# RG-LRU heads in pairs with 64x64 gate products, and mLSTM chunks with grouped products, in a two-layer mixer trunk

## The chip, the cores and the metric

One NeuronCore of a Trainium2 chip runs the whole program. The metric is the device time of one execution in microseconds (us). PE is the matrix engine (its weight loads are listed as PEld), DVE the vector engine, ACT the scalar engine, POOL and SP issue DMAs. Each engine runs its instructions in the order that the build fixed.

## The reference

A trunk of two layers over 768 tokens (256 of context, 512 latent), width 1024, in float32. In each layer one projection feeds three bidirectional mixers (HGRN2, mLSTM, RG-LRU), whose outputs are gated, merged, projected and followed by a SwiGLU FFN. The change lies in the RG-LRU (8 blocks of 64 features) and in the mLSTM (4 heads), both cut here:

```
def rglru(xc, r_pre, i_pre, lam, h0):
    log_a = -LRU_C * jax.nn.softplus(-lam) * jax.nn.sigmoid(r_pre)
    a = jnp.exp(log_a)
    u = jnp.sqrt(jnp.maximum(-jnp.expm1(2.0 * log_a), 0.0)) * (jax.nn.sigmoid(i_pre) * xc)
    a_cum, h = lax.associative_scan(_linear_combine, (a, u), axis=1)
...
    xc = depthwise_conv(lru_x, conv_w, conv_b).astype(f32)
    gates = jnp.einsum('btnd,zgnde->zgbtne', xc.reshape(bsz, t, LRU_BLOCKS, LRU_BD),
                       lru_gate_w.astype(f32)).reshape(N_DIR, 2, bsz, t, LRU_W)
...
        log_d = jnp.where(mask, b[..., :, None] - b[..., None, :] + ic[..., None, :], NEG_BIG)
...
        s = jnp.einsum('bhtk,bhsk->bhts', qc, kc) * jnp.exp(log_d - m_row[..., None])
        w_inter = jnp.exp(log_inter - m_row)
        num = s @ vc + w_inter[..., None] * (qc @ c_mem)
        den = jnp.sum(s, axis=-1) + w_inter * jnp.einsum('bhtk,bhk->bht', qc, n_mem)
        h = num / jnp.maximum(jnp.abs(den), jnp.exp(-m_row))[..., None]
...
    b_out = head_rms_norm(h_ml, ml_norm_w) * jax.nn.sigmoid(ml_o.astype(f32))
    c_out = h_lru * jax.nn.gelu(lru_y.astype(f32))
```

## The kernel before

Activations are kept feature-major, 128 features by 768 tokens. A dense product takes its weights from DRAM (SP's queue, 512 KB a panel), splits them into a high part on ACT (`split_w`, L210) and a low part on DVE (L212), and runs three PE products per 128 rows (L386 for the mixers' projections, L496 token-major, L1050 in the later stages) in one of four accumulation banks of PSUM (`acc`). Two banks (`mx`) and two more (`pl`) serve the mixers. In a layer the stages follow as: HGRN2 heads, RG-LRU heads (`lru(i)`, four of 128 features), mLSTM gates and log-decays (`mg`), mLSTM head pairs (`mlstm(0)`, `mlstm(1)`), branches, output, FFN. The framework's scheduler fixes the order of each engine at build time by its own estimates, and mixes work of neighbouring stages: projections of the next stage stand on PE between the small products of the one before. Buffers are rings by tag (`BUFS`), and the order of an instruction among others follows from what it reads and from `high_priority`.

`lru(i)` projects x (L788), convolves it on DVE (L791, L795), fills a 128x128 block-diagonal tile with two 64x64 blocks per direction and gate (a memset, two DMAs), and multiplies: per direction and gate one product of 512 and one of 256 columns (L808), each emptied by a sigmoid on ACT (L809). Then Exp (L815), Tanh (L816) and Sqrt (L824) on ACT, each from another function table, multiplications (L817, L819, L820, L825) and the scans (L827, L829, L830) on DVE, and the gelu of y.

`mg` projects values and gates, transposes the gates (L885), scans them over time on DVE (L888 to L892), and transposes three results to columns (L923); the first waits for L900. Log-decays go to DRAM.

`mlstm(p)` treats two heads: keys weighed by column (L954), state products (L973, 64 columns each) and the states (L980). Then for each 128-token chunk: log-decays are loaded (`ub`), shifted and masked (L992) and exponentiated (L994); scores (L998, 64 rows) are weighed with them (L1001); for each head and direction a product of weighed scores and values (L1008, 128 rows) and one with the state (L1010, 64 rows) add up in a bank. ACT takes the absolute denominator (L1013) and scales (L1017), DVE does the rest (L1014, L1015, L1018). `head_norm_out` then normalizes each head over all chunks (L629 to L635), transposes (L640) and gates it.

## Time and profile before

| | |
|---|---|
| median of three runs | 2617.3 us (2615.47 to 2621.12) |
| the profiled execution | 2623.0 us, span 2621.2 us, mean granted clock 0.983 |
| PE busy | 2540.6 us, 97% of the span |
| DVE, ACT, POOL busy | 1573.5, 962.8, 111.1 us |
| chain that ended last | PE 49%, issue 4%, DVE 4%, DMA 1%, ACT 1% |

A line of the profile names an operation by its source line, its engine and the tiles that it writes and reads; L0lru_pl is a `pl` bank in layer 0's RG-LRU. A busy share says how full an engine is; what a change of one stage can move is read from the waits of that stage.

### The profile page before, as it was taken

The numbers are of one execution on the slowest core, as the hardware profiler recorded it, in microseconds if no ns is written. First come the engines' busy times: TensorE is split into PE (matmuls) and PEld (weight loads), VectorE is DVE, ScalarE is ACT, GpSimd is POOL, SyncE is SP. The second block draws the span as 40 slices with busy tenths as digits, with TensorE's granted clock in tenths as the row PEclk, the third lists the DMA queues.
The fourth block names the chain that finished last, engine by engine and source line by source line (L and its number), as shares of the span: only waits on it lengthen the run. The fifth ranks groups of instructions, "written<-read, shape, count | busy, mean of one in ns | idle before, by whom it ended". The sixth has DMA issues, their size and how long they took to land.

```text
span 2621.2 us, 36224 instructions
## 1 busy us (share of the span) xinstructions
PE 2540.6 (97%) x14491; PEld 2195.9 (84%) x14491; DVE 1573.5 (60%) x3007; ACT 962.8 (37%) x1470; POOL 111.1 (4%) x213
## 2 busy tenths in 40 slices
...
GB/s 243 57 48 54 46 69 65 75 77 105 142 128 114 120 121 145 112 99 167 113 103 139 51 139 65 57 55 64 63 80 122 112 105 176 114 97 97 97 91 111
DMA packets 247480, 264.42 MB, mean 101 GB/s; under 512 B 12328, under 2 KB 213360, under 8 KB 247312
## 3 DMA queue, kind: packets, MB, share of 16 engines
...
## 4 chain that ended last, share of the span: by engine, by line
PE 49%; issue 4%; DVE 4%; DMA 1%; ACT 1%; POOL 0%; ACTq 0%; DVEq 0%; POOLq 0%
PE L0ffn_acc L1050 18%; PE L1ffn_acc L1050 14%; PE L1br_acc L1050 5%; PE L1hg_acc L386 4%; PE L1mg_acc L496 1%; PE L1hg_pl L707 1%; PE L1ml_acc L386 1%; PE L1lru_acc L386 1%; PE L1out_acc L1050 1%; PE L1v_acc L496 1%; PE L1lru_pl L808 0%; PE L1ml_mx L1010 0%; DVE L0ffn_h L377 0%; PE L1hg_mx L746 0%; DMA L1hg_w<-in_w_in_dram 0%
## 5 line engine op out<-in xcount | busy, mean ns | idle before, releaser
L1050 PE MATMUL L0ffn_acc<-L0out_h,L0ffn_wh 128*128 128x256 f32 (+1 forms) x1408 | 349.3, 340 | 6.7 <-DVE L0out_h L377 3.0
L1050 PEld LDWEIGHTS L0ffn_acc<-L0out_h,L0ffn_wh 128*128 128x128 f32 x1408 | 242.0, 190 | 39.1 <-DVE L0out_h L377 4.4
L1050 PE MATMUL L0ffn_acc<-L0out_h,L0ffn_wl 128*128 128x256 f32 (+1 forms) x704 | 236.4, 337 | 0.0
L1050 PE MATMUL L1ffn_acc<-L1out_h,L1ffn_wh 128*128 128x512 f32 (+1 forms) x736 | 219.7, 381 | 1.8 <-ACT L1out_h L376 0.9
L258 DVE SCALAR_TENSOR_TENSOR ada_ny<-ada_w,csk,ada_ny 128x512 f32<-128x512 f32 x224 | 157.8, 749 | 74.9 <-DMA ada_w<-in_w_ada_dram 73.9
L1050 PE MATMUL L0br_acc<-h,L0br_wh 128*128 128x512 f32 (+1 forms) x768 | 191.3, 340 | 0.3 <-DVE L0br_gt L1099 0.3
L210 ACT ACTIVATE L0ffn_wh<-L0ffn_w 128x1024 fp32r<-128x1024 f32 (+1 forms) x76 | 77.3, 1017 | 278.4 <-PE L0ffn_acc L1050 250.6
L212 DVE TENSOR_TENSOR L1ffn_wl<-L1ffn_w,L1ffn_wh 128x1024 fp32r<-128x1024 f32 (+1 forms) x76 | 88.8, 1169 | 142.2 <-ACT L1ffn_wh L210 141.3
L1050 PE MATMUL L0ffn_acc<-L0ffn_hid,L0ffn_wh 128*128 128x256 f32 (+1 forms) x704 | 172.5, 337 | 0.0
L1050 PEld LDWEIGHTS L1ffn_acc<-L1out_h,L1ffn_wh 128*128 128x128 f32 x736 | 136.2, 188 | 28.8 <-DVE L1out_h L377 1.5
L210 ACT ACTIVATE L1ffn_wh<-L1ffn_w 128x1024 fp32r<-128x1024 f32 (+1 forms) x76 | 77.4, 1018 | 197.5 <-PE L1ffn_acc L1050 156.8
L212 DVE TENSOR_TENSOR L0ffn_wl<-L0ffn_w,L0ffn_wh 128x1024 fp32r<-128x1024 f32 (+1 forms) x68 | 81.1, 1192 | 111.6 <-ACT L0ffn_wh L210 111.1
L1050 PEld LDWEIGHTS L0br_acc<-h,L0br_wh 128*128 128x128 f32 x768 | 131.9, 190 | 17.3 <-DVE L0br_gt L1099 0.5
L1050 PEld LDWEIGHTS L0ffn_acc<-L0out_h,L0ffn_wl 128*128 128x128 f32 x704 | 133.4, 190 | 14.3
L1050 PE MATMUL L1ffn_acc<-L1out_h,L1ffn_wl 128*128 128x512 f32 (+1 forms) x368 | 139.4, 380 | 0.0
L386 PE MATMUL L0hg_acc<-h,L0hg_wh 128*128 128x384 f32 (+2 forms) x512 | 136.1, 343 | 0.0
L1050 PEld LDWEIGHTS L0ffn_acc<-L0ffn_hid,L0ffn_wh 128*128 128x128 f32 x704 | 121.0, 190 | 14.2
L1050 PE MATMUL L0br_acc<-h,L0br_wl 128*128 128x256 f32 (+1 forms) x384 | 129.5, 337 | 0.0
L1050 PE MATMUL L1br_acc<-L0ffn_h,L1br_wh 128*128 128x512 f32 x384 | 121.0, 393 | 1.5 <-ACT L1br_gt L1069 1.5
L1050 PE MATMUL L1ffn_acc<-L1ffn_hid,L1ffn_wh 128*128 128x512 f32 (+1 forms) x448 | 115.2, 346 | 0.0
L386 PE MATMUL L1hg_acc<-L0ffn_h,L1hg_wh 128*128 128x384 f32 (+1 forms) x384 | 107.8, 359 | 0.0
L1050 PE MATMUL L0ffn_acc<-L0ffn_hid,L0ffn_wl 128*128 128x256 f32 (+1 forms) x304 | 102.2, 336 | 0.0
(707 smaller groups left out, 5932.4 us busy)
## 6 DMA issues: line engine op xcount, KB each, us to landing
...
```

The lines of the kernel that those rows point to most:

```text
L210: ACT.activation(wh[:, :n], w[:, :n], AF.Copy)
L212: V.tensor_tensor(wl[:, :n], w[:, :n], wh[:, :n].bitcast(F32), op=OP.subtract)
L258: V.scalar_tensor_tensor(ac[i], wv, csk[:, kk, i:i + 1], ac[i], op0=OP.mult, op1=OP.add)
L386: PE.matmul(ps[:, :n], A[:, k, :], B[k][:, off - ao:off - ao + n], start=(i == 0), stop=(i == 3 * nk - 1))
L496: PE.matmul(ps[:, :n], A[k][:, c * 128:(c + 1) * 128], W[:, k % 4, :], start=k == 0 and i == 0, stop=k == 7 and i == 3 * (k1 - k0) - 1)
L707: PE.matmul(pv[:, j * 128:(j + 1) * 128], ks[:, j * 128:(j + 1) * 128], comp(Q[g], c, j, j + 1), start=True, stop=True)
L1050: PE.matmul(ps[:, :n], A[:, k, sl], Bm[k0 + k][:, off - ao:off - ao + n], start=cnt[key] == 0, stop=cnt[key] == tot - 1)
```

## The change

`lru` now takes two heads. Pair (0,1) stands where the four heads stood, pair (2,3) behind `mg` and ahead of the mLSTM. The 64x64 gate blocks are multiplied as such: for the first gate two products on the diagonal quadrants of the array, for the second two on the other two, with the conv's output whose halves two DMAs have swapped (`xs`); both gates of a direction and column group have a bank. All sigmoids of a pair come first, then Exp, Tanh and squares, then Sqrt (`behind` fixes the order without a wait). a² and a step of the gelu go from DVE to ACT.

In `mlstm` the weights of three chunks are prepared ahead in tiles of other tags; the 64-row state products of both heads are written ahead of the 128-row products, and the next chunk's scores between them; the absolute value and the scaling go from ACT to DVE; each head is normalized in two halves, the first while later chunks run. The tile P becomes T wide.

```
+    def behind(ins, other):
+        tc.add_manual_dep(ins.ins, other.ins.name, mybir.DependencyInfo(mybir.DependencyClass.NoSync, mybir.DependencyReason.DATA),
+                          reason="issue order")
...
+                xs = S("kt")
+                wg = S("th", 256).rearrange("p (z c) -> p z c", z=4)
+                for b in range(2):
+                    ldg(xs[64 * b:64 * b + 64], xc[64 - 64 * b:128 - 64 * b])
+                    for z in range(2):
+                        ldg(wg[64 * b:64 * b + 64, z::2, :], gw[:, z, 2 * i + (1 - b if z else b)].rearrange("d n e -> n d e"))
+                sg[i] = [[S(t) for t in ts] for ts in ((("K", "K"), ("K", "K")), (("P", "P"), ("z", "Q")))[k]]
+                for d in range(2):
                     for off, n in ALL:
-                        ps = pl()
-                        PE.matmul(ps[:, :n], wg[:, 2 * d + z], xc[:, off:off + n], start=True, stop=True)
-                        ACT.activation(sg[d][z][:, off:off + n], ps[:, :n], AF.Sigmoid, bias=vec[l]["gate_b"][:, bi:bi + 1])
+                        pz = [pl() for z in range(2)]
+                        for b in range(2):
+                            PE.matmul(pz[0][64 * b:64 * b + 64, :n], wg[64 * b:64 * b + 64, 2 * d], xc[64 * b:64 * b + 64, off:off + n],
+                                      start=True, stop=True)
+                        for b in range(2):
+                            PE.matmul(pz[1][64 - 64 * b:128 - 64 * b, :n], wg[64 * b:64 * b + 64, 2 * d + 1], xs[64 * b:64 * b + 64, off:off + n],
+                                      start=True, stop=True)
+                        for z in range(2):
+                            bi = (d * 2 + z) * 4 + i
+                            last = ACT.activation(sg[i][d][z][:, off:off + n], pz[z][:, :n], AF.Sigmoid, bias=vec[l]["gate_b"][:, bi:bi + 1])
...
+                    behind(ACT.activation(av, s_r, AF.Exp, scale=nsp8[l][:, d * 4 + i:d * 4 + i + 1]), last)
+                    behind(ACT.activation(s_r, s_r, AF.Tanh, scale=sp8[l][:, d * 4 + i:d * 4 + i + 1]), last)
...
+                    behind(ACT.activation(s_r, s_r, AF.Sqrt), tanh)
...
-        for i in range(4):
-            lru(i)
+        lru((0, 1))
...
+        lru((2, 3))
...
+                ub = S(("P", "P", "z")[i % 3])
...
+            def heads(c, pt, nxt):
+                ix = [ORD[d].index(c) - 1 for d in range(2)]
+                ds = [d for d in range(2) if ix[d] >= 0]
+                pos = [mx() for b in range(2)]
+                for d in ds:
+                    for b in range(2):
+                        PE.matmul(pos[b][:, d * 129:(d + 1) * 129], wb[d][64 * b:64 * b + 64, c * 128:(c + 1) * 128],
+                                  cst[d][64 * b:64 * b + 64, ix[d], :], start=d == ds[0], stop=False)
+                sc = scores(nxt) if nxt is not None else None
                 for b in range(2):
...
+                        PE.matmul(po[:, d * 129:(d + 1) * 129], pt[:, k * 128:(k + 1) * 128], mv[c][:, 2 * p + b, :],
+                                  start=False, stop=d == 1)
...
-                    ACT.activation(rd, po[:, 0:258].rearrange("p (d v) -> p d v", v=129)[:, :, 128], AF.Abs)
+                    V.scalar_tensor_tensor(rd, den, -1.0, rd, op0=OP.mult, op1=OP.max)
-                    ACT.activation(o, po[:, 0:128], AF.Identity, scale=rd[:, 0:1])
+                    V.tensor_scalar(o, po[:, 0:128], rd[:, 0:1], None, op0=OP.mult)
...
+            ubs = {c: weights(i, c) for i, c in enumerate(chs[:3])}
+            sc = scores(chs[0])
+            for i, c in enumerate(chs):
+                pt = weigh(sc, ubs.pop(c))
+                if i + 3 < len(chs):
+                    ubs[chs[i + 3]] = weights(i, chs[i + 3])
+                sc = heads(c, pt, chs[i + 1] if i + 1 < len(chs) else None)
+                if c == half:
+                    head_norm(hsl, "mn", zt_, chs[0], half)
```

The change shifts most line numbers; those that the prediction speaks of are: gate products L808, now L817 (first gate) and L820 (second); sigmoids L809, now L824; Sqrt L824, now L856; scans L827 to L830, now L859 to L862; column transposes L923, now L944; keys L954, now L977; state products L973, now L996; scores L998, now L1024; state and value products of a chunk L1010 and L1008, now L1042 and L1049; output transposes L640, now L646; projections L386 and L1050, now L390 and L1106; weight split L212, now L216.

The order on PE where layer 0's second RG-LRU head multiplies its gates, before and after (F is the conv's output, kt the swapped one, th the weights, acc a projection's bank):

```order
L386 MATMUL L0lru_acc_3557<-h_149,L0lru_wh_3552 128x512
L808 MATMUL L0lru_pl_3314<-L0lru_F_3300,L0lru_th_3308 128x512
L808 MATMUL L0lru_pl_3317<-L0lru_F_3300,L0lru_th_3308 128x256
L386 MATMUL L0lru_acc_3557<-h_157,L0lru_wh_3552 128x512
L386 MATMUL L0lru_acc_3557<-h_149,L0lru_wl_3553 128x512
L808 MATMUL L0lru_pl_3320<-L0lru_F_3300,L0lru_th_3308 128x512
L808 MATMUL L0lru_pl_3323<-L0lru_F_3300,L0lru_th_3308 128x256
L386 MATMUL L0lru_acc_3557<-h_150,L0lru_wh_3552 128x512
L386 MATMUL L0lru_acc_3557<-h_158,L0lru_wh_3552 128x512
L808 MATMUL L0lru_pl_3328<-L0lru_F_3300,L0lru_th_3308 128x512
L808 MATMUL L0lru_pl_3331<-L0lru_F_3300,L0lru_th_3308 128x256
L386 MATMUL L0lru_acc_3557<-h_150,L0lru_wl_3553 128x512
```

```order
L390 MATMUL L0lru_acc_3303<-h_155,L0lru_wl_3273 128x256
L390 MATMUL L0lru_acc_3303<-h_156,L0lru_wh_3272 128x256
L817 MATMUL L0lru_pl_3237<-L0lru_F_3217,L0lru_th_3226 64x512
L646 MATMUL L0hg_mx_3036<-ident,L0hg_o_2991 128x128 x4
L646 MATMUL L0hg_mx_3042<-ident,L0hg_o_2991 128x128 x2
L817 MATMUL L0lru_pl_3237<-L0lru_F_3217,L0lru_th_3226 64x512
L820 MATMUL L0lru_pl_3238<-L0lru_kt_3225,L0lru_th_3226 64x512 x2
L817 MATMUL L0lru_pl_3245<-L0lru_F_3217,L0lru_th_3226 64x256 x2
L390 MATMUL L0lru_acc_3303<-h_164,L0lru_wh_3272 128x256
L390 MATMUL L0lru_acc_3303<-h_156,L0lru_wl_3273 128x256
L390 MATMUL L0lru_acc_3340<-h_149,L0lru_wh_3335 128x512
L820 MATMUL L0lru_pl_3246<-L0lru_kt_3225,L0lru_th_3226 64x256 x2
```

Two products of one gate stood together, then projections; now a group is two or four quadrants, its parts apart in places by projections and by transposes of HGRN2.

The order on PE in a chunk of layer 0's `mlstm(1)` (mx is the chunk's bank, sd a state, K its weights, Q the weighed scores, v the values):

```order
L1008 MATMUL L0ml_mx_5258<-L0mg_v_3808,L0ml_Q_5251 128x129
L1010 MATMUL L0ml_mx_5258<-L0ml_sd_5096,L0ml_K_5090 128x129
L1008 MATMUL L0ml_mx_5258<-L0mg_v_3808,L0ml_Q_5251 128x129
L1010 MATMUL L0ml_mx_5258<-L0ml_sd_5120,L0ml_K_5114 128x129
L1008 MATMUL L0ml_mx_5269<-L0mg_v_3808,L0ml_Q_5251 128x129
L1010 MATMUL L0ml_mx_5269<-L0ml_sd_5096,L0ml_K_5090 128x129
L1008 MATMUL L0ml_mx_5269<-L0mg_v_3808,L0ml_Q_5251 128x129
L1010 MATMUL L0ml_mx_5269<-L0ml_sd_5120,L0ml_K_5114 128x129
L998 MATMUL L0ml_pl_5288<-L0ml_q_4837,L0ml_F_4838 128x128
L998 MATMUL L0ml_pl_5291<-L0ml_q_4837,L0ml_F_4838 128x128
```

```order
L1042 MATMUL L0ml_mx_5341<-L0ml_sd_5162,L0ml_K_5156 128x129
L1042 MATMUL L0ml_mx_5341<-L0ml_sd_5186,L0ml_K_5180 128x129
L1049 MATMUL L0ml_mx_5341<-L0mg_v_3450,L0ml_Q_5337 128x129 x2
L1106 MATMUL L0br_acc_5544<-h_155,L0br_wl_5514 128x512
L1106 MATMUL L0br_acc_5544<-h_156,L0br_wh_5513 128x512
L1106 MATMUL L0br_acc_5544<-h_164,L0br_wh_5513 128x512
L1106 MATMUL L0br_acc_5544<-h_156,L0br_wl_5514 128x512
L1042 MATMUL L0ml_mx_5395<-L0ml_sd_5162,L0ml_K_5156 128x129
L1042 MATMUL L0ml_mx_5395<-L0ml_sd_5186,L0ml_K_5180 128x129
L1049 MATMUL L0ml_mx_5395<-L0mg_v_3451,L0ml_Q_5392 128x129 x2
L1106 MATMUL L0br_acc_5557<-h_153,L0br_wh_5513 128x256
L1106 MATMUL L0br_acc_5557<-h_161,L0br_wh_5513 128x256
```

The 128-row and the 64-row products alternated for two heads; now a head's two 64-row ones stand ahead of its two 128-row ones, and projections of the next stage stand between the heads.

The order on DVE ahead of the first weighed keys of layer 1's `mlstm(0)` (L954 before, L977 after; scans are printed there as SCALAR_TENSOR_TENSOR):

```order
L907 TENSOR_TENSOR L1mg_Q_16784<-L1mg_K_16767,L1mg_mp_16773 64x768
L914 TENSOR_TENSOR L1mg_K_16745<-L1mg_K_16744,L1mg_ul_16781 64x768
L212 TENSOR_TENSOR L1ml_wl_17242<-L1ml_w_17240,L1ml_wh_17241 128x1024
L924 COPY L1mg_col_16807<-L1mg_mx_16808 128x384
L924 COPY L1mg_col_16816<-L1mg_mx_16817 128x384
L212 TENSOR_TENSOR L1ml_wl_17274<-L1ml_w_17272,L1ml_wh_17273 128x1024
L943 TENSOR_SCALAR L1ml_th_16917<-L1ml_th_16917 128x512
L992 SCALAR_TENSOR_TENSOR L1ml_Q_17050<-L1ml_Q_17050,L1mg_col_16798,mlmask 128x128 x4
L212 TENSOR_TENSOR L1ml_wl_17334<-L1ml_w_17332,L1ml_wh_17333 128x1024
L943 TENSOR_SCALAR L1ml_th_16918<-L1ml_th_16918 128x512
L954 TENSOR_TENSOR L1ml_K_16996<-L1ml_kt_16985,L1mg_col_16807 128x768
L954 TENSOR_TENSOR L1ml_K_16998<-L1ml_kt_16985,L1mg_col_16807 128x768
```

```order
L859 SCALAR_TENSOR_TENSOR L1lru_Q_16921<-L1lru_Q_16921,L1lru_P_16796 128x768
L216 TENSOR_TENSOR L1ml_wl_17434<-L1ml_w_17432,L1ml_wh_17433 128x1024
L863 TENSOR_TENSOR L1lru_Q_16905<-L1lru_Q_16905,L1lru_F_16912 128x512
L857 TENSOR_TENSOR L1lru_Q_16798<-L1lru_Q_16798,L1lru_z_16797 128x768
L864 SCALAR_TENSOR_TENSOR L1lru_o_16831<-L1lru_o_16831,L1lru_Q_16905 128x512
L216 TENSOR_TENSOR L1ml_wl_17494<-L1ml_w_17492,L1ml_wh_17493 128x1024
L861 SCALAR_TENSOR_TENSOR L1lru_F_16928<-L1lru_F_16928,L1lru_Q_16798 128x256
L966 TENSOR_SCALAR L1ml_th_17049<-L1ml_th_17049 128x512
L862 SCALAR_TENSOR_TENSOR L1lru_F_16928<-L1lru_F_16928,L1lru_Q_16798 128x512
L966 TENSOR_SCALAR L1ml_th_17050<-L1ml_th_17050 128x512
L863 TENSOR_TENSOR L1lru_Q_16921<-L1lru_Q_16921,L1lru_F_16928 128x512
L977 TENSOR_TENSOR L1ml_K_17128<-L1ml_kt_17117,L1mg_col_16591 128x768
```

Ahead of the keys stood the column copies and the first log-decays; now the second pair's last scans and multiplications (L857 to L864) stand there.

## Rows read from the trace of the kernel before

**Rows 1.** Windows, both mixer stages: busy us by engine, PEclk, DMA
```profile
280.00:600.00 320.00, 299.78 (x1761) 249.32 (x1760) 223.74 (x478) 150.13 (x239) 28.01 (x52) 0.95 0.35 65
1750.00:2020.00 270.00, 258.04 (x1425) 207.79 (x1424) 200.63 (x435) 145.44 (x220) 28.15 (x53) 0.97 0.49 77
```

**Rows 2.** Waits of PE, 280:600 and 1750:2020: total us, times, longest
```profile
PE L0ml_mx L640 <- DVE L0ml_o L635: 7.1, 2, 6.7
PE L0ml_mx L1008 <- DVE L0ml_Q L1001: 5.8, 2, 3.7
PE L0mg_mx L923 <- DVE L0mg_K L900: 3.8, 1, 3.8
...
PE L1lru_pl L808 <- ACT L1lru_K L809: 4.0, 2, 2.9
PE L1mg_mx L923 <- DVE L1mg_K L900: 3.8, 1, 3.8
```

**Rows 3.** Windows of four slices of 20 us, with the granted clock
```profile
500.00:520.00 20.00, 20.00 (x91) 15.40 (x89) 7.76 (x28) 5.38 (x15) 1.58 (x3) 0.76 0.24 53
580.00:600.00 20.00, 10.66 (x36) 8.12 (x37) 10.85 (x31) 5.56 (x12) 1.26 (x3) 0.57 0.33 47
1820.00:1840.00 20.00, 17.07 (x70) 12.91 (x69) 12.65 (x16) 14.37 (x19) 1.76 (x3) 0.83 0.38 56
1900.00:1920.00 20.00, 16.22 (x82) 13.81 (x81) 12.28 (x18) 6.17 (x8) 6.67 (x12) 0.83 0.53 97
```

**Rows 4.** Timeline of PE: start, us; xcount counts records, two a product
```profile
315.72 1.02 PE L808 MATMUL L0lru_pl<-L0lru_F,L0lru_th 128*128 128x512 f32 x2
316.58 0.49 PE L729 MATMUL L0hg_mx<-ident,L0hg_K 128*128 128x128 f32 x3
...
543.83 1.32 PE L973 MATMUL L0ml_mx<-L0mg_v,L0ml_K 128*64 128x129 f32 x20
...
567.26 0.39 PE L1050 MATMUL L0br_acc<-h,L0br_wl 128*128 128x512 f32 x1
567.49 0.62 PE L1050 MATMUL L0br_acc<-h,L0br_wh 128*128 128x512 f32 x2
...
568.51 0.49 PE L1010 MATMUL L0ml_mx<-L0ml_sd,L0ml_K 64*128 64x129 f32 x2
568.92 0.49 PE L1008 MATMUL L0ml_mx<-L0mg_v,L0ml_Q 128*128 128x129 f32 x2
...
571.01 0.37 PE L1010 MATMUL L0ml_mx<-L0ml_sd,L0ml_K 64*128 64x129 f32 x1
571.02 0.37 PE L998 MATMUL L0ml_pl<-L0ml_q,L0ml_F 64*128 64x128 f32 x1
```

**Rows 5.** Timeline at the end of layer 0's second mLSTM pair
```profile
589.54 0.84 ACT L629 ACTIVATE L0ml_K<-L0ml_o 128x768 f32<-128x768 f32 x1 [0.42 <-DVE L0ml_o L1018]
...
590.42 0.95 DVE L630 TENSOR_REDUCE L0ml_mnred<-L0ml_K 128x6 f32<-128x768 f32 x1 [0.91 <-ACT L0ml_K L629]
```

**Rows 6.** ACT's lines by form, 280:400: busy us, mean ns
```profile
L809 ACT ACTIVATE L0lru_K<-L0lru_pl,vec 128x512 f32<-128x512 f32 x15 | 10.4, 692 | 1.5 <-PE L0lru_pl L808 0.9
L815 ACT ACT_TABLE_LOAD x7 | 9.0, 1283 | 0.1
...
L816 ACT ACTIVATE L0lru_K<-L0lru_K,sp 128x768 f32<-128x768 f32 x7 | 6.6, 936 | 0.0
L210 ACT ACTIVATE L0lru_wh<-L0lru_w 128x1024 fp32r<-128x1024 f32 x6 | 6.3, 1058 | 7.7 <-PE L0lru_acc L386 5.6 <-PE L0hg_acc L386 2.1
```

**Rows 7.** Lines of DVE by form, the same stretch
```profile
L212 DVE TENSOR_TENSOR L0lru_wl<-L0lru_w,L0lru_wh 128x1024 fp32r<-128x1024 f32 x6 | 7.3, 1212 | 0.0
L817 DVE TENSOR_TENSOR L0lru_K<-L0lru_K,L0lru_F 128x768 f32<-128x768 f32 x7 | 6.7, 954 | 3.4 <-ACT L0lru_K L809 3.4
...
L827 DVE TENSOR_TENSOR_SCAN L0lru_Q<-L0lru_Q,L0lru_K 128x768 f32<-128x768 f32 x3 | 5.3, 1753 | 0.0
```

**Rows 8.** DMA issues: count, KB each, median us to landing
```profile
st_d<-L0lru_o POOLq DMA_DIRECT2D x4, 384.0 KB, 3.8
```

More of the change, by code (lines that the diff above doesn't have):

```diff
@@ L593, in layer @@
         G.memset(rst[32:64].rearrange("p (c t) -> p c t", t=128)[:, :, 127:128], 0.0)
-        Pm = [[S("P", 384).rearrange("p (c t) -> p c t", t=128) for g in range(2)] for i in range(2)]
+        Pm = [S("P").rearrange("p (g c t) -> p g c t", g=2, t=128) for i in range(2)]
+        Pm = [[P_[:, g] for g in range(2)] for P_ in Pm]
         for i in range(2):
```

184 lines of the change are left out of this document (95 added, 89 removed), and 2 rows, old and new, of the table BUFS.

## The prediction

> **What bounds the kernel now.** I read the stretches first: the two mixer stages (280 to 600 us in layer 0, 1750 to 2020 us in layer 1) hold every line of the change, and PE is busy 299.78 of 320 and 258.04 of 270 us there [rows 1]. So PE sets the time, and what can be won is its idle 20.2 + 12.0 = 32.2 us, its low clock, and its work. The waits of PE name the idle time [rows 2]: in layer 0 6.7 us in one piece before the output transposes (L640, for DVE's L635), 5.8 us before the value products of the mLSTM (L1008, for the weighing L1001), 3.8 us before the column transposes (L923, for the scans that end in L900); in layer 1 4.0 us before the RG-LRU gate products (L808, for the sigmoids L809) and again 3.8 us at L923. The clock comes third, in slices of 20 us [rows 3]: after such a wait it falls to its lower level of 1.2 GHz for a while. At 0.76 a slice with PE busy for all 20.00 us has lost 4.8 us; at 0.57, 0.83 and 0.83 the slices lost at least 3.9, 1.9 and 1.5 us (20 times the missing share, less half of the slice's idle time). ACT and DVE are busy about half and three quarters of these stretches, and matter only where PE waits for them.
>
> **PE's own work.** A gate product of 512 columns takes PE 0.86 us from start to start (315.72 to 316.58) [rows 4], one of 256 half of it. The 64 of them (8 heads, 2 directions, 2 gates, 2 column groups) come to 8 x 4 x (0.86 + 0.43) = 41.3 us. The change makes them 128 quadrants. Halves of the array do run side by side here: twenty records (ten products, each 64 columns wide) of L973 fill 1.32 us, where ten in a row at 0.22 would take 2.2; and a row half of L1010 and one of L998 start 0.01 us apart [rows 4]. No row shows quadrants. The bounds are 20.6 us (four abreast all the time) and 82.6 (one after another). In the order of the changed program they stand in 37 groups, many of two, because the list of PE puts projections or HGRN2 products between a gate's two halves; four abreast where four stand together, two where two do, gives 33.5 us, which I take because both kinds of halves do it: 7.8 us less. One rule speaks against it: the Trainium skill, "TensorEngine Tiling (Array Packing)", Restrictions and Gotchas, Gotcha 1, says that different row tiles cannot use one PSUM bank at the same time, as a gate's two quadrants do. By that rule the gate products would cost between 41.3 and 82.6 us, and the sum would rise by 7.8 to 49 us (a rival, below); no row here shows it or excludes it. A change of tile shape costs about 0.2 us: L1008 and L1010 in turns start every 0.41 us (568.51, 568.92) [rows 4], where a quarter of the 0.86 us, 0.22, is its length. The mLSTM's grouping takes 44 such changes away, the quadrants add 74: 251 become 281, 30 x 0.2 = 6.0 us. All in all PE's work falls by **1.6 us** (0.2 us go to 64-row products that no longer overlap). The heads of a chunk are not merged in most places: a head's two 64-row products stand together, then its two 128-row ones, then projections.
>
> **RG-LRU waits.** Functions by table: 56 table loads become 21, 35 x 1.28 us [rows 6] = 45 us off ACT. ACT is not the bound, so this buys only the waits that ACT's backlog caused: the 4.0 us of layer 1. In exchange the sigmoids must empty two banks per gate and column group: 2 x 0.69 us for 512 columns [rows 6] against 0.86 on PE, so where gate groups stand nearly back to back, as in the pairs (2,3), ACT sets their pace. I leave 1.2 of the 4.0: **-2.8 us**, and the low clock behind it, **-1.9** [rows 3]. The second gate's products wait for halves of the conv's output swapped by two DMAs; a store of 384 KB there takes 3.8 us to land [rows 8], and POOL issues them. In the order 0.4 to 5 us of other PE work stand between the first gate's products and the second's; if every first product waited for the conv, the rest would be some 13 us in all, and 0 if PE comes late. The conv ends well ahead in most heads: **+1.0**. The column group's four small weight loads and the missing memset lie on POOL (4% busy) and cost nothing.
>
> **Scans between the pairs.** The first L923 waits 3.8 us in each layer. In the changed order pair (2,3)'s projections, not the mLSTM's, stand between the forget gates' transposes and this first column transpose, and there are hardly more of them: 6.6 us against 5.9. On DVE the same five scans of up to 1.75 us [rows 7] stand ahead, with only a small eviction less. So the wait stays, 0.7 us shorter in each layer: **-1.4**, and the low clock behind it stays.
>
> **mLSTM.** The 5.8 us at L1008 come from log-decays that land or are weighed just in time. Three chunks ahead, they are there long before, and 1.0 is left: **-4.8**. With it goes the low clock at 500 to 520 us, **-4.8**, and half of that at 580 to 600 us, **-2.0** [rows 3]. The 6.7 us at the end of pair 1 are a chain: square, reduction, reciprocal root, multiplication, of which 0.84 and 0.95 us [rows 5] and about 0.95 for the multiplication now do half; the order still has the transposes right behind the last value product, with nothing between. **-1.4**. ACT's small steps move to DVE in each chunk, off the chain and cheap.
>
> **The new wait.** Pair (2,3)'s tail now lies in front of the mLSTM. Walk layer 1 from the last gate product, in the order of the changed program. ACT, up to its first square root: 13 full-width functions at 0.94, 7 narrower ones at 0.69 or less, 3 weight splits at 1.06, 2 table loads at 1.28 [rows 6], 22.6 us. Then DVE up to the first keys of the mLSTM (L977): 4 multiplications and L977 itself at 0.95, 4 scans at 1.75, 2 splits at 1.21 [rows 7], 5 narrower steps at some 0.64: 17.4 us. With 0.9 us for the product and its sigmoid, 40.9 us. PE has until its first use of L977 (L996) 129 projections of 512 columns at 0.23 [rows 4], 24 of half that and a few transposes, 34.9 us. PE waits **6.0 us**. In layer 0 the same walk gives 50.3 against 47.5 us: **3.0**. Such waits bring the low clock, by the smaller rows 1.5 to 1.9 us each [rows 3]: **+3.5**. If ACT or DVE is ahead of this walk the cost is 0; if each step there comes late, twice as much.
>
> **The sum.** Gains: 1.6 + 2.8 + 1.9 + 1.4 + 4.8 + 4.8 + 2.0 + 1.4 = 20.7. Costs: 1.0 + 6.0 + 3.0 + 3.5 = 13.5. Net 7.2 us off the profiled 2623.0 us, 2615.8. That execution stands 5.7 us above the median of the runs (2617.3), so I forecast **2610 us**. A measurement of this kernel can tell about 0.2% (5.2 us) from no change: faster is under 2612.1, slower over 2622.5. The forecast's own range is 2602 to 2620.
>
> **Rivals.**
> - *The new wait doesn't come.* If ACT's queue is ahead of my walk, the 12.5 us of wait and clock are saved, and perhaps the 4 us that I leave at L640 and L923: 2594 to 2598. For it: the 45 us off ACT. Against: the walk uses only what must run in order. With the remaining low clock gone, too, 2580.
> - *The change doesn't do what it says.* The order shows the heads hardly merged and the scans hardly covered. If the weights ahead also miss (their tiles are freed only by the tail of the RG-LRU), 4.8 + 2.0 + some of 4.8 stay: 2612 to 2620, no change.
> - *Quadrants that don't run abreast.* The nearest rows are halves. The price is in the gate products: two abreast at most, 41.3 us instead of 33.5, 2618; one after another, 82.6, 2659. It decides from 46 us on, when fewer than 1.8 run abreast on average: then slower. For it: no row shows four, and a gate's two quadrants share a bank across the row halves, which L1010 and L998 (two banks) don't. That is the case of the rule named above (the Trainium skill, "TensorEngine Tiling (Array Packing)", Gotcha 1). Against: the column halves of L973 share a bank and overlap.
> - *A longer tail, slower than before.* Place: L996 at the start of mlstm(0). If ACT's evictions for the projections wait behind the Exp, Tanh and Sqrt of two heads, PE also loses accumulation banks, and the 12.5 us double: 2623 or more. It decides when waits and clock there pass 25 us. For it: DVE is busy 200 of 270 us in layer 1 [rows 1]. Against: four accumulation banks of 24 projections at 0.23 us each are some 20 us of slack.
>
> **How the numbers follow.** Forecast 0.42 (0.24 of it under 2612, the rest no change); the new wait doesn't come 0.24, faster; the change doesn't do what it says 0.07, no change; quadrants at most two abreast 0.08 (0.02 slower), one after another 0.07, slower; a longer tail 0.12, slower. Faster 0.48, same 0.31, slower 0.21. The range of 2586 to 2630 leaves out the serial quadrants, the best of the second case and the worst of the last, some 0.14.
>
> **What would show it.** In the changed kernel's waits: L996 for DVE's L977, 6 us in layer 1 and 3 in layer 0; L944 (formerly L923) still near 3 us twice; L1049 (formerly L1008) near nothing; L646 (formerly L640) above 5. In the timeline four quadrants that start within some 0.05 us and end together would confirm 33.5 us; starts 0.4 or 0.86 us apart would refute it. Tables: 21 loads on ACT. I am wrong if PE's idle in the two stretches falls under 20 us (then much faster) or passes 40.

## The result, and the profile of the changed kernel

The change makes the kernel slower: 2656.95 us (median of four runs, 2655.44 to 2661.69) against 2617.19, a ratio of 1.0151 with the 95% interval 1.0135 to 1.0167. The prediction said 2610 us, and its range ended at 2630. In what follows a ratio is always to runs of the kernel before on the same chip and in the same job (medians 2619.6 to 2623.0 us); 0.001 of it is 2.6 us.

The head of the changed kernel's profile (busy us, share of the span, instructions). PE is 8.2 us busier than before, where the prediction said 1.6 less:

```profile
span 2655.1 us, 36510 instructions
...
PE 2548.8 (96%) x14619; PEld 2176.7 (82%) x14619; DVE 1570.7 (59%) x3127; ACT 915.2 (34%) x1387; POOL 124.2 (5%) x237
```

Windows of the changed kernel (columns as in [rows 1]; the granted clock is the third number from the end): both mixer stages, the second one longer now, then slices of 20 us that answer to [rows 3]:

```profile
280.00:600.00 320.00, 298.70 (x1825) 235.50 (x1823) 217.51 (x525) 126.65 (x188) 32.82 (x60) 0.96 0.36 67
1750.00:2060.00 310.00, 282.16 (x1563) 215.38 (x1562) 204.50 (x500) 127.77 (x195) 35.92 (x67) 0.93 0.45 76
420.00:440.00 20.00, 12.90 (x46) 7.01 (x45) 6.41 (x12) 4.50 (x6) 2.09 (x4) 0.73 0.31 67
440.00:460.00 20.00, 19.14 (x87) 9.01 (x86) 4.45 (x5) 11.97 (x20) 0.00 (x0) 0.76 0.00 0
500.00:520.00 20.00, 19.21 (x122) 14.32 (x121) 15.63 (x44) 2.48 (x5) 2.28 (x3) 1.00 0.56 113
600.00:620.00 20.00, 14.48 (x69) 12.33 (x70) 8.46 (x23) 4.58 (x8) 3.26 (x6) 0.74 0.62 144
1900.00:1920.00 20.00, 19.09 (x80) 7.84 (x81) 4.44 (x5) 12.16 (x20) 0.00 (x0) 0.82 0.13 16
```

From its first HGRN2 projection to the end of the mLSTM, layer 0's mixer takes 8 us longer than before, layer 1's 28 to 29. At 420 to 440 us PE is busy for 12.90 of 20 us at a clock of 0.73, a mean of its two levels, 1.00 (2.4 GHz) up to 428 us and 0.50 (1.2 GHz) from 430 us on; the mLSTM's slice at 500 to 520, 0.76 before, is at 1.00. The wait that stood at 580 to 600 us before is found at 600 to 620 (14.48 of 20, clock 0.74); behind the waits of L996 in layer 1 the clock is 0.82 (1900 to 1920).

PE's waits in the changed kernel (total us, times, longest), layer 0 (280 to 600), then layer 1 (1750 to 2060); they answer to [rows 2]:

```profile
PE L0lru_pl L820 <- DMA L0lru_kt<-L0lru_F: 11.2, 2, 7.1
PE L0mg_mx L944 <- DVE L0mg_P L921: 3.9, 1, 3.9
...
PE L0ml_mx L996 <- DVE L0ml_K L977: 0.8, 1, 0.8
...
PE L1lru_pl L820 <- DMA L1lru_kt<-L1lru_F: 6.8, 2, 4.7
PE L1ml_mx L646 <- DVE L1ml_o L638: 5.9, 1, 5.9
PE L1mg_mx L944 <- DVE L1mg_P L921: 3.9, 1, 3.9
PE L1ml_mx L996 <- DVE L1ml_K L977: 2.8, 1, 2.8
PE L1ml_mx L996 <- DVE L1ml_mdec L985: 2.5, 1, 2.5
PE L1ml_mx L996 <- DVE L1ml_F L1003: 1.8, 1, 1.8
```

New and largest is L820, the second gate's products, for the DMA that swaps the halves of the conv's output: 11.2 + 6.8 = 18.0 us. The scans' wait stands as before (L944, 3.9 and 3.9), L1049 (the former L1008, 5.8 us) is gone, and L996 is there as forecast, in layer 1 in three parts, 7.1 us. In the two stretches PE is idle for 21.3 + 27.8 = 49.1 us, past the 40 that the prediction gave as its sign of being wrong.

What L820 waits for shows in the changed kernel's DMA issues (queue, count, KB each, median us from issue to landing) and in the timeline at two heads (PE, and POOL's issue of the copy):

```profile
L0lru_kt<-L0lru_F POOLq DMA_DIRECT2D x8, 192.0 KB, 7.7
...
L1lru_kt<-L1lru_F POOLq DMA_DIRECT2D x8, 192.0 KB, 5.7
```

```profile
335.02 0.65 PE L817 MATMUL L0lru_pl<-L0lru_F,L0lru_th 64*64 64x512 f32 x2
335.04 0.65 PE L820 MATMUL L0lru_pl<-L0lru_kt,L0lru_th 64*64 64x512 f32 x2
335.50 0.60 PE L817 MATMUL L0lru_pl<-L0lru_F,L0lru_th 64*64 64x512 f32 x2
335.52 0.59 PE L820 MATMUL L0lru_pl<-L0lru_kt,L0lru_th 64*64 64x512 f32 x2
336.04 0.50 PE L390 MATMUL L0lru_acc<-h,L0lru_wl 128*128 128x512 f32 x1
...
423.38 1.08 PE L817 MATMUL L0lru_pl<-L0lru_F,L0lru_th 64*64 64x512 f32 x4
423.61 1.06 POOL L112 DMA_DIRECT2D L0lru_kt<-L0lru_F  x2 [3.82 <-DVE L0lru_F L805]
...
426.57 0.28 PE L390 MATMUL L0lru_acc<-h,L0lru_wh 128*128 128x256 f32 x1
433.95 1.11 PE L820 MATMUL L0lru_pl<-L0lru_kt,L0lru_th 64*64 64x512 f32 x1 [7.10 <-DMA L0lru_kt<-L0lru_F]
```

First the good case, at 335 us: two quadrants of the first gate and two of the second start within 0.02 us (335.02, 335.04), their second records at 335.50 and 335.52, and a projection follows at 336.04. Two gate products of 512 columns take 1.02 us, where two full ones take 1.72 [rows 4]. Then the bad case: the first gate's quadrants run at 423.38, as soon as the conv is done; projections fill until 426.57, and then PE stands for 7.10 us, until the swapped copy has landed. POOL issued its two DMAs from 423.61 to 424.67, right behind the conv. It was not late; PE's wait ended at 433.95, 9.3 us after the issues. The good case is the second direction of a pair's first head, whose copy has long landed; the two waits of each layer stand at the first direction of that head, one in each pair.

### The profile page after: what moved, and what is told of

Its sections match the earlier page's. It is cut to its first block, busy times and chain, and to the rows that moved or that the text cites. A ratio compares the mean times of both kernels' runs of the same rounds, so it can differ in the third digit from the quotient of the medians.

```text
span 2655.1 us, 36510 instructions
## 1 busy us (share of the span) xinstructions
PE 2548.8 (96%) x14619; PEld 2176.7 (82%) x14619; DVE 1570.7 (59%) x3127; ACT 915.2 (34%) x1387; POOL 124.2 (5%) x237
## 4 chain that ended last, share of the span: by engine, by line
PE 48%; issue 5%; DVE 4%; DMA 2%; ACT 2%; POOL 0%; POOLq 0%; ACTq 0%; DVEq 0%
PE L0ffn_acc L1106 17%; PE L1ffn_acc L1106 13%; PE L1br_acc L1106 4%; PE L1hg_acc L390 4%; PE L1mg_acc L500 1%; PE L1lru_acc L390 1%; PE L1hg_pl L713 1%; PE L1out_acc L1106 1%; PE L1v_acc L500 1%; PE L1lru_pl L820 1%; DMA L1lru_kt<-L1lru_F 1%; DVE ada_ny L262 0%; DVE L0ffn_h L381 0%; PE L1ml_acc L390 0%; DMA L1br_zt<-L0ffn_d 0%
## 5 line engine op out<-in xcount | busy, mean ns | idle before, releaser
L1106 PE MATMUL L0ffn_acc<-L0out_h,L0ffn_wh 128*128 128x256 f32 (+1 forms) x1408 | 349.7, 340 | 5.8 <-DVE L0out_h L381 3.0
L1106 PEld LDWEIGHTS L0ffn_acc<-L0out_h,L0ffn_wh 128*128 128x128 f32 x1408 | 242.8, 191 | 38.4 <-DVE L0out_h L381 4.4
L1106 PE MATMUL L0ffn_acc<-L0out_h,L0ffn_wl 128*128 128x256 f32 (+1 forms) x704 | 237.0, 338 | 0.0
L1106 PE MATMUL L1ffn_acc<-L1out_h,L1ffn_wh 128*128 128x512 f32 (+1 forms) x736 | 219.9, 381 | 1.8 <-ACT L1out_h L380 0.9
L1106 PE MATMUL L0br_acc<-h,L0br_wh 128*128 128x512 f32 (+1 forms) x768 | 192.3, 341 | 0.0
L216 DVE TENSOR_TENSOR L1ffn_wl<-L1ffn_w,L1ffn_wh 128x1024 fp32r<-128x1024 f32 (+1 forms) x76 | 88.8, 1168 | 142.0 <-ACT L1ffn_wh L214 141.2
L1106 PE MATMUL L0ffn_acc<-L0ffn_hid,L0ffn_wh 128*128 128x256 f32 (+1 forms) x704 | 172.7, 337 | 0.0
L1106 PEld LDWEIGHTS L1ffn_acc<-L1out_h,L1ffn_wh 128*128 128x128 f32 x736 | 136.3, 188 | 28.8 <-DVE L1out_h L381 1.5
L1106 PEld LDWEIGHTS L0br_acc<-h,L0br_wh 128*128 128x128 f32 x768 | 132.9, 191 | 16.5 <-issue 0.2
L1106 PEld LDWEIGHTS L0ffn_acc<-L0out_h,L0ffn_wl 128*128 128x128 f32 x704 | 133.8, 191 | 14.1
L216 DVE TENSOR_TENSOR L0ffn_wl<-L0ffn_w,L0ffn_wh 128x1024 fp32r<-128x1024 f32 (+1 forms) x68 | 80.9, 1190 | 108.1 <-ACT L0ffn_wh L214 107.8
L1106 PE MATMUL L1ffn_acc<-L1out_h,L1ffn_wl 128*128 128x512 f32 (+1 forms) x368 | 139.5, 380 | 0.0
L390 PE MATMUL L0hg_acc<-h,L0hg_wh 128*128 128x384 f32 (+2 forms) x512 | 136.2, 343 | 0.0
L1106 PEld LDWEIGHTS L0ffn_acc<-L0ffn_hid,L0ffn_wh 128*128 128x128 f32 x704 | 121.0, 190 | 14.2
L1106 PE MATMUL L0br_acc<-h,L0br_wl 128*128 128x256 f32 (+1 forms) x384 | 130.2, 339 | 0.0
L1106 PE MATMUL L1br_acc<-L0ffn_h,L1br_wh 128*128 128x512 f32 x384 | 123.2, 400 | 0.0
L1106 PE MATMUL L1ffn_acc<-L1ffn_hid,L1ffn_wh 128*128 128x512 f32 (+1 forms) x448 | 115.3, 346 | 0.0
L390 PE MATMUL L1hg_acc<-L0ffn_h,L1hg_wh 128*128 128x384 f32 (+1 forms) x384 | 107.9, 360 | 0.0
L1106 PE MATMUL L0ffn_acc<-L0ffn_hid,L0ffn_wl 128*128 128x256 f32 (+1 forms) x304 | 102.4, 337 | 0.0
```

Of the source, the lines that this page charges most:

```text
L216: V.tensor_tensor(wl[:, :n], w[:, :n], wh[:, :n].bitcast(F32), op=OP.subtract)
L390: PE.matmul(ps[:, :n], A[:, k, :], B[k][:, off - ao:off - ao + n], start=(i == 0), stop=(i == 3 * nk - 1))
L1106: PE.matmul(ps[:, :n], A[:, k, sl], Bm[k0 + k][:, off - ao:off - ao + n], start=cnt[key] == 0, stop=cnt[key] == tot - 1)
```

## Experiments: which half of the change

**The mLSTM half alone**: the new `mlstm`, with the old `lru(i)`, four heads ahead of `mg`.

```
-        lru((0, 1))
+        for i in range(4):
+            lru(i)          # the function of before
...
-        lru((2, 3))
```

> Only the mLSTM's half of the change (weights ahead, grouped products, steps moved to DVE, norm in halves); the RG-LRU heads one by one ahead of the gates stage, as before. Theory A: without the swap and the moved pair the mLSTM's gains show, 2600 to 2608 us. Theory B, with the fault in the mLSTM's own DVE load: 2617 to 2630 us.

Measured: 2599.88 us, 0.9921 [0.9901, 0.9941]. Its waits of PE, layer 0, then layer 1:

```profile
PE L0ml_mx L646 <- DVE L0ml_o L638: 5.7, 1, 5.7
PE L0mg_mx L931 <- DVE L0mg_P L908: 3.8, 1, 3.8
...
PE L1lru_pl L816 <- ACT L1lru_K L817: 4.1, 2, 3.0
PE L1mg_mx L931 <- DVE L1mg_P L908: 3.8, 1, 3.8
```

This half wins 20.7 us. The weights ahead take away the L1008 waits; the scans' wait (here L931) and 5.7 us ahead of the output transposes stay, and the old RG-LRU's 4.1 us in layer 1 is there, too.

**The RG-LRU half alone**: the new `lru` in its new places, with the old `mlstm`.

> Only the RG-LRU's half of the change (pairs, quadrants, swap, tables, second pair behind the gates stage); the mLSTM as before. Theory A: the whole loss and a little more, 2650 to 2665 us, with the waits for the swap near 18 us. Theory B: the tail without the mLSTM's added DVE steps, 2630 to 2645 us.

Measured: 2676.8 us, 1.0216 [1.0177, 1.0256], with 11.7 us at the swapped copy in layer 0 and 5.8 in layer 1. That is more than theory A gave. The whole loss is in this half; the mLSTM takes back some 30% of it.

## Experiments: the swapped copy

**No copy.** Both gates on the two diagonal quadrants, both reading `xc`; the rest is the changed kernel.

```
-                xs = S("kt")
...
-                    ldg(xs[64 * b:64 * b + 64], xc[64 - 64 * b:128 - 64 * b])
...
-   PE.matmul(pz[1][64 - 64 * b:128 - 64 * b, :n], wg[...], xs[64 * b:64 * b + 64, off:off + n], ...
+   PE.matmul(pz[1][64 * b:64 * b + 64, :n], wg[...], xc[64 * b:64 * b + 64, off:off + n], ...
```

> The changed kernel with both gates of a head on the diagonal quadrants: the second gate's products read the conv's output itself, so the two swap DMAs are gone; at most two quadrants run abreast. Theory A (the second gate's products wait for the swap DMAs, 11.2 + 6.8 us in the changed kernel's waits, and the clock falls behind each wait): 18 us of waits go, some 6 us of low clock with them, 8 us come back because only two run abreast: about 2640 us. Theory B (the second pair's tail ahead of the mLSTM and DVE's load there made the loss): the swap's waits only moved to ACT and DVE, 2655 to 2665 us. Theory C (tile-shape changes by the quadrants made it): 2655 to 2665 us.

Measured: 2628.76 us, 1.0035 [1.0023, 1.0047]: 30 of the 40 us are gone with the copy, more than theory A gave. The run takes away two things, the copy and the four abreast that it serves; 30 us is the net of both. The two slices after 420 us read without it:

```profile
420.00:440.00 20.00, 20.00 (x108) 9.90 (x107) 8.13 (x13) 12.99 (x22) 0.00 (x0) 1.00 0.18 27
440.00:460.00 20.00, 20.00 (x112) 17.50 (x111) 13.64 (x15) 19.97 (x27) 0.00 (x0) 1.00 0.43 58
```

PE is busy for all 40 us there, at full clock. In the changed kernel the second of these slices has PE busy for 19.14 of 20 us and a clock of 0.76. So the copy costs twice, by the waits and by the low clock behind them.

**The copy on SP's queue** instead of POOL's (`ld` for `ldg`).

> The changed kernel with the swap's two DMAs on SP's queue in place of POOL's. If the time to landing (7.7 and 5.7 us) is made by POOL's queue: some 3 us sooner, PE's waits for the swap fall from 18 to some 8 us, 2642 to 2650 us. If it is the transfer of 64 partitions itself: as the changed kernel, 2653 to 2660 us. If the DMA stands behind waiting weight loads in SP's queue: later, over 2660 us.

Measured: 2669.95 us, 1.0181 [1.0152, 1.021]. The copies land after 5.8 us in layer 0 (7.7 on POOL's queue) and 7.4 in layer 1 (5.7). The time is that of the third forecast, but not for its reason alone: PE's waits for the copy hardly change (8.7 + 8.1 = 16.8 us for 18.0), and PE also waits 8.8 us in layer 0 for a sigmoid that writes the tile z, a wait that full products (below) bring, too. Another queue is no cure.

**Both pairs ahead of `mg`**, with and without the copy.

```
         lru((0, 1))
+        lru((2, 3))
...
-        lru((2, 3))
```

> The changed kernel with both pairs ahead of the gates stage; the quadrants and the swap DMAs stay. Theory A (the swap made most of the loss, the tail ahead of the mLSTM little): the waits for the swap stay near 18 us, only the 7 us at the state products of layer 1 and some low clock go, 2643 to 2652 us. Theory B (the tail matters more than the swap): 2630 us or less.

> The diagonal quadrants (no swap), 2629 us so far, with both pairs ahead of the gates stage. If the second pair's place behind the gates stage costs what the mLSTM's half has won: 2605 to 2612 us. If the pairs themselves cost it (sigmoids of two heads in a row on ACT, four banks' worth of evictions against PE): 2622 to 2630 us, and PE's waits lie in the gate products.

Measured: with the copy 2634.12 us, 1.0049 [1.0036, 1.0062]; without it 2620.4, 0.9991 [0.9979, 1.0003]. The first lies between its two theories; the second is nearest the one that blames the pairs, with PE's waits at the gate products, 2.9 + 3.4 us. Ahead of `mg` the copy costs 15 us, half as much, and there it lands sooner (with the copy):

```profile
L0lru_kt<-L0lru_F POOLq DMA_DIRECT2D x8, 192.0 KB, 3.9
...
L1lru_kt<-L1lru_F POOLq DMA_DIRECT2D x8, 192.0 KB, 3.3
```

The same 192 KB take 3.9 and 3.3 us here, 7.7 and 5.7 in the changed kernel. What slows them there is not settled. At the wait of 7.1 us a weight panel of 512 KB was on its way beside them, and the DMA engines were busy for 0.87 and 0.82 of the time (424 to 426, 426 to 428 us); no run takes that panel away.

## Experiments: quadrants, pairs, the place, and a tile

**Full products.** The 128x128 block-diagonal tile of before, one product per gate, all else as changed.

```
-                wg = S("th", 256).rearrange("p (z c) -> p z c", z=4)
+                wg = S("th", 512).rearrange("p (z c) -> p z c", z=4)
+                G.memset(wg, 0.0)
...
+   for z in range(2):
+       PE.matmul(pz[z][:, :n], wg[:, 2 * d + z], xc[:, off:off + n], start=True, stop=True)
```

> The changed kernel with the gate products as full 128x128 block-diagonal products, as before; pairs, tables, place of the pairs and the mLSTM stay changed. Theory A: no swap, no shape change at the gates; 2630 us or a little less than the diagonal quadrants. Theory B: 2650 to 2657 us, since the tail stays. Theory C: falls below the diagonal quadrants by some 15 us (74 shape changes at 0.2 us).

Measured: 2627.81 us, 1.0027 [1.0015, 1.0038], the same as diagonal quadrants. It looked as if quadrants cost nothing. The waits say otherwise (PE in layer 0's first pair and in layer 1, then ACT in layer 0's first pair):

```profile
PE L0lru_pl L816 <- ACT L0lru_z L819: 9.3, 1, 9.3
...
PE L1lru_pl L816 <- ACT L1lru_z L819: 7.6, 1, 7.6
...
ACT L0lru_z L819 <- DMA st_d<-L0hg_z: 10.0, 1, 10.0
```

PE waits 9.3 and 7.6 us for a sigmoid, and that sigmoid waits for the only tile of the tag z, which holds HGRN2's output until a DMA has stored it. Counted as below, the gate products come to 46.9 us here and to 65.5 with diagonal quadrants, and PE's waits at them to 16.9 and 5.7: of the 18.6 us that full products save on PE, 11.2 came back as waits.

**The old heads 2 and 3 behind `mg`**, one by one, with the new mLSTM.

> The mLSTM's half alone (2600 us), with heads 2 and 3 moved one by one behind the gates stage; products, tables and pairs as before. If the place alone costs: 2612 to 2625 us, with waits at the state products of layer 1. If it costs only together with the pairs' batched functions (a tail of two heads): 2597 to 2605 us. The wait for the scans at the column transposes, 3.8 us a layer, stays in both cases.

Measured: 2627.28 us, 1.0018 [1.0003, 1.0033], 25 us above the same code ahead of `mg` by the ratios. Its waits of PE, layer 0, then layer 1:

```profile
PE L0ml_mx L984 <- DVE L0ml_F L991: 4.2, 1, 4.2
...
PE L1ml_mx L984 <- DVE L1ml_sd L991: 6.4, 1, 6.4
PE L1ml_mx L646 <- DVE L1ml_o L638: 5.7, 2, 4.5
PE L1lru_pl L816 <- ACT L1lru_K L817: 4.9, 1, 4.9
```

The state products (L984) wait for states, in layer 0 for 4.2 us, where the changed kernel has 0.8. By this run alone the place would cost 25 us; the pairs with full products and two z tiles (below) lose no such time there. Why the old heads are so slow there stays open.

**Single heads or pairs, quadrants or full products, all ahead of `mg`**: three runs that make a square with the one above (0.9991). Single heads are the changed function, called for one head at a time:

```
-        lru((0, 1))
-        lru((2, 3))
+        for i_ in range(4):
+            lru((i_,))
```

> The changed kernel with both gates on the diagonal quadrants (no swapped copy) and all four RG-LRU heads ahead of mg, but each head alone (all its sigmoids, then its Exp, Tanh, squares, then Sqrt), not in pairs. With pairs this was 2620.4 us; with the old RG-LRU code in the same place and the new mLSTM it was 2599.9. Theory P (the pairing costs these 20 us: the functions of a head wait until both heads' gates are through, and mg begins 11 and up to 20 us later): 2600 to 2606. Theory Q (the quadrants cost them): 2615 to 2622, with the pairs of full products (next run) at 2600 to 2606. Theory F (the order of functions within a head and the squares moved to ACT cost them): 2615 to 2622 here and in both other runs.

> The changed kernel with full 128x128 block-diagonal gate products (no quadrants, no swapped copy), both pairs ahead of mg. Theory P (pairing): 2615 to 2622, as with diagonal quadrants. Theory Q (quadrants): 2600 to 2606. Theory F: 2615 to 2622.

> Full 128x128 gate products, four single heads ahead of mg: what is left of the change in the RG-LRU is the order of functions within a head (two banks of gates at a time, all sigmoids first, Sqrt last) and the two squares on ACT. Theory P and theory Q: 2598 to 2606, as the old RG-LRU code with the new mLSTM. Theory F: 2615 to 2622.

| ahead of `mg` | heads in pairs | single heads |
|---|---|---|
| diagonal quadrants | 2620.4 us, 0.9991 [0.9979, 1.0003] | 2608.47 us, 0.9959 [0.9944, 0.9974] |
| full products | 2603.45 us, 0.9934 [0.992, 0.9949] | 2594.59 us, 0.9898 [0.9881, 0.9914] |

Theories P and Q are both half right: by the ratios the pairing costs 8 to 9 us, the quadrants 15 to 16. Theory F falls: the new order of the functions wins some 6 us against the old code (0.9921), though the two intervals overlap. The last run beats the kernel before by 1.0% and the changed kernel by 2.5%. Its head, to be read against the changed kernel's above:

```profile
span 2593.4 us, 36222 instructions
...
PE 2523.6 (97%) x14491; PEld 2183.5 (84%) x14491; DVE 1572.6 (61%) x3127; ACT 928.0 (36%) x1397; POOL 111.3 (4%) x213
```

What the pairing costs is in part a matter of tiles. A single head writes its four sigmoids to tiles of the tag K; the second head of a pair writes them to P, z and Q, and both tiles of the tag o go to one pair's outputs. With full products, pairs ahead of `mg`:

```profile
PE L1lru_pl L816 <- ACT L1lru_o L825: 4.9, 1, 4.9
...
ACT L1lru_o L825 <- DMA L0ffn_d<-L1lru_o: 7.3, 1, 7.3
```

In layer 1 ACT waits 7.3 us until a DMA has stored an output of the pair before, and PE behind it 4.9 us. In layer 0 PE waits 1.8 us for z, which holds HGRN2's output until it is stored, and 3.1 us that the profile puts down to no one and that end just behind the conv's last step on DVE. In all PE waits 10.0 us at the gate products of the pairs and 0.5 at those of the single heads, about the difference in time. No run has pairs ahead of `mg` with more tiles of z and o, so what pairs cost without these waits is open.

Why quadrants cost shows in PE's timeline of the single heads with quadrants:

```profile
1776.51 0.28 PE L390 MATMUL L1lru_acc<-L0ffn_h,L1lru_wl 128*128 128x256 f32 x1
1776.63 0.29 PE L390 MATMUL L1lru_acc<-L0ffn_h,L1lru_wh 128*128 128x256 f32 x1
1776.84 0.65 PE L818 MATMUL L1lru_pl<-L1lru_F,L1lru_th 64*64 64x256 f32 x4
1777.33 1.02 PE L815 MATMUL L1lru_pl<-L1lru_F,L1lru_th 64*64 64x512 f32 x2
1778.28 0.49 PE L769 MATMUL L1hg_mx<-L0ffn_v,L0ffn_P 128*128 128x128 f32 x2
```

Projection records of 256 columns follow each other after 0.12 us; the four quadrant records behind them start after 0.21. Then one quadrant of 512 columns stands alone (two records) and holds PE for 0.95 us, until 1778.28, longer than a full product's 0.86 [rows 4]. Diagonal quadrants can win nothing: both gates use the same two, and two abreast do what one full product does. For all gate products of both layers, from the start of the record ahead of each unbroken group to the start of the first record behind it, less PE's waits in them, I count 45.1 us in the kernel before (42 groups), 45.4 in the best run above, 63.3 with single heads and quadrants, and 69.8 in the changed kernel (37 groups). With both pairs ahead of `mg` it is 67.4 us for four quadrants with the copy and 66.8 for diagonal ones: the second pair of quadrants saved nothing that shows.

**Two z tiles**, in the kernel with full products at the changed kernel's place.

```
-    "q": 2, ... "z": 1, "v": 6,
+    "q": 2, ... "z": 2, "v": 6,
```

> The run of full 128x128 gate products at the changed kernel's place (pair (2,3) behind mg; 2627.8 us), with two tiles of the tag z instead of one. There the gate products of pair (0,1) waited 9.3 and 7.6 us, once in each layer, for a sigmoid that writes the single z tile, which the HGRN2 output normalisation still holds; and the gate products took PE 39.3 us from start to start, the diagonal quadrants at the same place 54.5 us, for the same total time. Theory W (what the full products save on PE was given back in this wait): the wait goes and the time falls by 12 to 17 us, to 2611 to 2616. Theory N (the tail of pair (2,3) ahead of the mLSTM sets the time there, and work ahead of it changes nothing): 2625 to 2629, with the wait reappearing at the scans' column transposes or the state products.

Measured: 2606.36 us, 0.9933 [0.9917, 0.995], 25 us less by the ratios, more than theory W gave. (The second tile also serves HGRN2's outputs, the scans of `mg` and the mLSTM's weights.) The pairs ahead of `mg`, with one z tile, have 0.9934. So the place behind `mg` and the second tile come out even together; the place by itself was not run. Waits of PE in layer 1:

```profile
PE L1mg_mx L939 <- DVE L1mg_P L916: 3.9, 1, 3.9
PE L1ml_pl L1019 <- DVE L1ml_Q L1028: 3.8, 1, 3.8
PE L1ml_mx L991 <- DVE L1ml_K L972: 2.8, 1, 2.8
```

The waits for the tail of pair (2,3) do come (L991, the products on the weighed keys, 2.8 us; L1019, the scores behind them, 3.8), beside the scans' wait. In exchange the 10.0 us at the gate products of the pairs ahead of `mg` are gone: here PE waits for nothing there.

**Two z tiles with quadrants**, diagonal ones and as changed.

> The run of diagonal quadrants at the changed kernel's place (2628.8 us), with two z tiles. Theory QP (quadrants cost PE 14 to 17 us wherever they stand, and this was hidden by the z tile's wait in the full products): the 5.7 us wait of layer 1 goes, with little else, 2619 to 2625, 13 to 18 above the full products with two z tiles (2606.4). Theory T (the single z tile was the whole cost of the place, and quadrants cost nothing once it is gone): 2604 to 2610.

> The changed kernel, nothing else than two z tiles. Theory S (the swapped copy and the quadrants cost it its 40 us; the sigmoids there wait for PE and not for the z tile): 2651 to 2658, no change. Theory T (the z tile is the cause): 2630 to 2636.

Measured: diagonal quadrants 2613.46 us (2612.92 to 2623.35), 0.997 [0.9957, 0.9982]. That lies between the theories: quadrants cost some 10 us there by the ratios (0.997 less 0.9933), less than the 15 to 16 ahead of `mg`. The changed kernel with two z tiles: 2663.28 us, 1.0162 [1.0143, 1.018]. Theory S holds, the tile is not the cause of the changed kernel's loss; PE waits for the copy as before (both layers):

```profile
PE L0lru_pl L820 <- DMA L0lru_kt<-L0lru_F: 9.6, 2, 5.4
...
PE L1lru_pl L820 <- DMA L1lru_kt<-L1lru_F: 6.2, 2, 4.1
```

These two runs also show how the copy's price is made up. Their profiled executions are 47.5 us apart (2670.9 and 2623.35). PE waits 21.7 us at the gate products in the one and not at all in the other; the clock, span times missing share, gives 2669.1 x 0.025 = 66.7 against 2621.5 x 0.016 = 41.9 us, 24.8 more. Together 46.5. This is an estimate: it leaves out some 8 us more of PE's waits elsewhere, and it counts the low clock also where PE stood idle.

## Why the prediction was wrong, step by step

The runs can be put in a row from the kernel before to the changed one, each with one thing more, but for the fourth row, which brings the place and the second z tile at once; the us are the ratio's steps times 2617:

| step | ratio | us |
|---|---|---|
| the new mLSTM | 0.9921 | -20.7 |
| RG-LRU functions in the new order, single heads, full products | 0.9898 | -6.0 |
| heads in pairs | 0.9934 | +9.4 |
| pair (2,3) behind `mg`, and two z tiles | 0.9933 | -0.3 |
| diagonal quadrants | 0.9970 | +9.7 |
| four quadrants with the swapped copy | 1.0162 | +50.2 |
| one z tile: the change | 1.0151 | -2.9 |

The steps depend on the order in which they are taken: with one z tile throughout, the place costs 24 us, the quadrants 2 and the copy 30.

- **The swapped copy, +1.0 (bounds 0 to 13): the step that failed.** With the four abreast that it serves, it cost 30 us at its place, 50 with two z tiles, 15 ahead of `mg`; PE's waits for it alone, 18.0 us, pass the bound of 13. Three things were wrong in it. The landing time came from a store, 3.8 us [rows 8]; the copies took 7.7 and 5.7. "The conv ends well ahead in most heads" is not so at the first head of each pair: there the first gate's products start as the conv ends, and the copy can't start before that. And the term carried no low clock behind the wait, which the prediction did put on its other waits.
- **PE's gate products, -7.8 and 74 changes of shape at 0.2 us (14.8): mis-sized.** +7.0 was reckoned for both together, +24.7 measured (69.8 less 45.1). The 33.5 us stood for 2.5 quadrants abreast on average (82.6 / 33.5). In the changed kernel's trace, records that start within 0.05 us of one another come 11 times in fours, 6 times in threes, 75 times in twos, and 44 stand alone. Weighed by columns that is 1.8 abreast, and at 0.43 us a pass of 512 columns 45.8 us, an estimate from these counts: more than the 41.3 of full products. The rival "two abreast at most" came nearer in size; as a mechanism it is wrong, since four do start within 0.02 us. The prediction's sign for its 33.5 us (four starts within some 0.05 us) came, the price did not. The Trainium skill, "TensorEngine Tiling (Array Packing)", Restrictions and Gotchas, Gotcha 1, is not borne out by the rows at 335 us: a gate's two quadrants, in different row halves, write one bank at the same time. The rest of the 24.7 us lies in changes of shape and in products that run at the low clock; how much in each, the runs don't tell.
- **RG-LRU waits, -2.8 and -1.9.** PE still waits for sigmoids in the changed kernel, 1.4 + 0.8 us in layer 0 and 0.8 + 0.6 in layer 1, 3.6 for the 4.0 of before. With full products and single heads 0.5 us of all waits at the gate products is left, so the function order does what it should, and the table loads did fall from 56 to 21; with pairs, waits for the tiles o and z come in.
- **Scans between the pairs, -1.4.** The wait stays, as reasoned; it is 3.9 us twice, not 0.7 shorter.
- **mLSTM: right as a sum.** L1008, the clock, L640 and 44 changes of shape less were reckoned at 4.8 + 4.8 + 2.0 + 1.4 + 8.8 - 0.2 = 21.6 us; the half alone wins 20.7. Its terms were not measured one by one, so that they add up so well may be luck in part. Within it the 5.7 us at the output transposes stay, now at 600 to 620 us, with their low clock.
- **The new wait at L996, 6.0 and 3.0.** Near in layer 1 as a sum (7.1), but only 2.8 us of it are for the keys of L977, to which the walk led; too much in layer 0 (0.8; the walk's 50.3 less 47.5 gives 2.8, not 3.0). With full products and two z tiles such waits come, too, and the kernel is no slower than with the pairs ahead of `mg` and one tile.
- **The rival "a longer tail", 2623 or more**, names another place; the loss lies ahead of it, in the gate products.

Not in the prediction at all: the price of the pairing (8 to 9 us), and the tiles z and o, for which ACT can now hold up PE.
